# Sliding-window copy: twelve staged batches for eleven, engines offset by fours, last stores in parts

## The chip, the cores and the metric

The kernel runs on one core of one Trainium2 chip. The metric is device time in microseconds; the median of six runs before the change is 752.82 us (751.74 to 755.47). No arithmetic is done at all: the kernel only moves data, so the parts of the chip that matter are the sixteen DMA engines of the core, the HBM, and three queues from which DMAs are issued: SP's (q1 in the profile), ACT's (q10) and GpSimd's, called POOL (q0).

## The reference

```python
batch, length, dim = (32, 4096, 256)          # x, float32; window_size = 64, stride = 32
n_windows = (length - window_size) // stride + 1      # 127
result = np.zeros((batch, n_windows, window_size, dim), dtype=np.float32)
for i in range(n_windows):
    start = i * stride
    result[:, i] = x[:, start:start + window_size].copy()
```

A batch of x is 128 blocks of 32 rows, 32 KB each (4.194 MB). Window i is blocks i and i+1, 64 KB, so neighbouring windows overlap by half, and each block but the first and the last of a batch is written twice: as the second half of one window and as the first half of the next. The output is 32 x 127 windows, 266.3 MB.

## The kernel before

There are two ways to make a batch's windows.

**Direct** copies go from x to the output, DRAM to DRAM, each block read twice. `Copier.windows` (L34) copies n windows, whole (64 KB each, in pieces of 32 KB) or one half of each. SP issues groups of sixteen windows, seven groups to a batch. Such a group is sent either as one DMA of whole windows or as a pair of DMAs, all first halves and then all second halves. The bytes are the same; with pairs the queue holds one completion packet to each piece of 32 KB, with whole windows one to two.

**Staged** batches are read once into an SBUF tile of 128 partitions, one block to a partition (`Copier.load`, L51, 4.194 MB in pieces of 16 KB), and stored twice from there (`Copier.store`, L61), once as first halves and once as second halves. Each store writes 128 halves where a batch has only 127 windows, so one half at each edge falls into the neighbouring batch: its window there must be written again afterwards. `Staging` has six tiles in turn. `Staging.run` on ACT issues up to six loads, then their twelve stores, then the next group; a load waits for the stores that leave its tile, a store for its load. The staged batches are 1, 4, 7 and so on to 31, eleven; 31 is shifted by one block, so that it spills only backwards, into two windows of batch 30.

The loop over `direct` sends 147 groups on SP. A small calculation sets whether a group goes as a pair: `turns` counts packets of the queue, four for a pair and three for a whole group, and `share` adds 90/120 of a pair while ACT's turn number lies among the loads and 12/120 while it lies among the stores. Windows that don't make up a group of sixteen are the edges: 15 to a batch, on the side next to a staged batch, sent by POOL. POOL waits until the third last group on SP has landed (semaphore `near`) and, for each edge, until the staged neighbour's stores have landed (`wait_stored`). It ends with four windows and nine more as `columns` (L44, pieces of 4 KB, spread over all engines). SP's own last copy is `columns` for windows 125 and 126 of batch 30, which waits for all stores of the last staged batch. Then SP waits for all copies.

Of the kernel before, what the change touches and what calls it, by code (L numbers as in the profile page):

```python
# [11 lines left out]
class Copier:  # L12
# [36 lines left out]
    def load(self, q, t, b, shift):  # L49

        return q.dma_start(  # L51
            out=t[:, :],
            in_=self.xap(b * self.nb - shift, [[self.blk, self.nb], [1, self.blk]]),
            max_dma_last_dim=IN,
        )

    def store(self, q, t, b, half, shift):


        w = b * self.nw - half - shift  # L60
        return q.dma_start(  # L61
            out=self.oap(2 * w + half, [[2 * self.blk, self.nb], [1, self.blk]]),
            in_=t[:, :],
            max_dma_last_dim=OUT,
        )


class Staging:


    def __init__(self, c, tc, pool, dtype, batches, bufs, shifts):
        self.c, self.batches, self.shifts = c, batches, shifts
        self.tiles = [pool.tile([128, c.blk], dtype, name=f"xb{i}") for i in range(bufs)]
        self.loaded = [tc.alloc_semaphore(f"loaded{i}") for i in range(bufs)]
        self.stored = [tc.alloc_semaphore(f"stored{i}") for i in range(bufs)]

    def shift(self, g):
        return self.shifts.get(self.batches[g], 0)

    def load(self, q, g):  # L80
        n, i = divmod(g, len(self.tiles))
        if n:
            q.wait_ge(self.stored[i], 32 * n)
        self.c.load(q, self.tiles[i], self.batches[g], self.shift(g)).then_inc(self.loaded[i], 16)

    def store(self, q, g):
        n, i = divmod(g, len(self.tiles))
        q.wait_ge(self.loaded[i], 16 * (n + 1))
        for half in (0, 1):
            self.c.store(q, self.tiles[i], self.batches[g], half, self.shift(g)).then_inc(self.stored[i], 16)  # L90

    def wait_stored(self, q, g):
        n, i = divmod(g, len(self.tiles))
        q.wait_ge(self.stored[i], 32 * (n + 1))  # L94

    def run(self, q):
        bufs = len(self.tiles)
        for first in range(0, len(self.batches), bufs):
            group = range(first, min(first + bufs, len(self.batches)))
# [7 lines left out]
def kernel(  # L107
# [13 lines left out]
    staged = [*range(1, B, 3)]  # L121
    direct = [b for b in range(B) if b not in staged]
    pool = ctx.enter_context(tc.tile_pool(name="xb", bufs=1))

    st = Staging(c, tc, pool, x.dtype, staged, 6, {0: -1, B - 1: 1})
# [10 lines left out]
    per, loads, stores = 6, 6 * 17, 34  # L138
    todo = 7 * len(direct)
    turns = share = 0  # L140
    with tc.tile_critical():  # L141
        st.run(ring_s)

        for b in direct:
            w = 0 if b - 1 not in staged else 8 if b + 1 in staged and b + 1 < B - 1 else 15
            for j in range(7):
                todo -= 1
                sem = near if todo == 2 else done
                share += 90 if turns % (loads + per * stores) < loads else 12
                if share >= 120:  # L150
                    share -= 120
                    turns += 4
                    count(c.windows(ring_d, b, w, 16, 0), done)
                    count(c.windows(ring_d, b, w, 16, 1), sem)
                else:
                    turns += 3
                    count(c.windows(ring_d, b, w, 16), sem)
                w += 16
                if todo == 7:
                    count(c.windows(ring_d, B - 1, c.nw - 1, 1, 1, 2048), done)  # L160
                    if 0 in staged:
                        count(c.windows(ring_d, 0, 0, 1, 0, 2048), done)

        ring_r.wait_ge(near, 16)
        pieces = (32768,)
        last = B - 2
        for i, b in enumerate(direct[:-1]):
# [51 lines left out]
```

## Time and profile before

| | |
|---|---|
| median of the runs | 752.82 us |
| the profiled execution | 752.34 us |
| its span, from the first to the last instruction | 750.6 us |
| DMA packets, bytes | 18098, 313.26 MB, mean 417 GB/s |
| stores on ACT: number, median from issue to landing | 22, 143.4 us |
| loads on ACT | 11, 124.6 us |
| direct copies on SP: whole groups, halves | 96, 102 |
| first load, and first direct copy, issued at | 0.91 and 0.96 us |
| POOL's edges: first issued, issued after the wait for a store | 653.3 us, 703.6 us |

The profile gives the span in 40 slices with the rate of the DMA engines in each; queue rows give packets, megabytes and the time that the packets took, as a share of sixteen engines. A row of the view by stretches has the stretch, its length, POOL's busy time, the clock, the DMA share and GB/s. Packets are counted where they start, so that short stretches can show a share above 1 or a rate of zero while the engines work on. Packets under 512 B are the completions that count up a semaphore.

### The profile page before, as it was taken

What the parts mean: (1) busy time and instruction counts of PE and PEld (TensorE: products, weight loads), DVE (VectorE), ACT (ScalarE), POOL (GpSimd) and SP (SyncE); (2) the same over time, 40 slices, a digit from 0 to 9 for tenths busy, and PEclk for the clock granted to TensorE, in tenths of its full rate; (3) what the DMA queues carried; (4) which work ended last, traced back from release to release, by engine and by line L of the source; (5) the groups of instructions that cost most, each with busy time, mean ns of one, the idle gap of its engine ahead of it and who ended that gap; (6) DMA issues with size and microseconds to landing.
All of it is one profiled execution on the core that took longest, in us unless ns stands there. A gap on an engine that the chain in (4) does not pass through costs nothing.

```text
span 750.6 us, 309 instructions
## 1 busy us (share of the span) xinstructions
POOL 12.7 (2%) x26
## 2 busy tenths in 40 slices
POOL 0000000000000000000000000000000000130100
DMA  9999999999999999999999999999999999999996
GB/s 370 424 427 419 428 428 418 422 426 424 417 422 419 423 417 420 425 421 417 414 417 417 418 428 429 432 424 424 435 422 424 417 422 431 418 423 426 421 417 269
DMA packets 18098, 313.26 MB, mean 417 GB/s; under 512 B 4144, under 2 KB 4144, under 8 KB 4336
## 3 DMA queue, kind: packets, MB, share of 16 engines
q1 hardware_dynamic: 7952, 154.32, 48.7%
q10 hardware_dynamic: 8976, 138.41, 44.1%
q0 software_dynamic: 1168, 20.51, 6.5%
q14 instruction: 2, 0.02, 0.0%
HBM read 220.95 MB, written 267.09 MB: 650 GB/s over the span
## 4 chain that ended last, share of the span: by engine, by line
another core or an unknown queue 92%; POOL 2%; issue 0%; POOLq 0%; SPq 0%
POOL out_dram L34 2%; POOL out_dram L44 0%; POOLq L214 0%; POOLq L94 0%; SPq L141 0%
## 5 line engine op out<-in xcount | busy, mean ns | idle before, releaser
L34 POOL DMA_DIRECT2D out_dram<-in_x_dram x21 | 12.0, 575 | 692.9 <-DMA out_dram<-in_x_dram 652.8
L44 POOL DMA_DIRECT2D out_dram<-in_x_dram x1 | 0.6, 581 | 0.0
L200 POOL MEMSET const-float32-0.0<- 128x1 f32 x1 | 0.1, 98 | 0.2 <-issue 0.2
L200 POOL MEMSET const-bfloat16-1.0<- 128x1 bf16 x1 | 0.1, 102 | 0.0
L200 POOL MEMSET const-float32-1.0<- 128x1 f32 x1 | 0.1, 98 | 0.0
L200 POOL MEMSET const-uint8-127<- 128x1 uint8 x1 | 0.1, 98 | 0.0
## 6 DMA issues: line engine op xcount, KB each, us to landing
out_dram<-in_x_dram SPq DMA_DIRECT2D x96, 1024.0 KB, 101.8
out_dram<-xb ACTq DMA_DIRECT2D x22, 4096.0 KB, 143.4
out_dram<-in_x_dram SPq DMA_DIRECT2D x102, 512.0 KB, 90.6
xb<-in_x_dram ACTq DMA_DIRECT2D x11, 4096.0 KB, 124.6
out_dram<-in_x_dram POOLq DMA_DIRECT2D x20, 960.0 KB, 39.2
out_dram<-in_x_dram POOLq DMA_DIRECT2D x1, 576.0 KB, 41.1
out_dram<-in_x_dram POOLq DMA_DIRECT2D x1, 256.0 KB, 38.6
out_dram<-in_x_dram SPq DMA_DIRECT2D x1, 128.0 KB, 2.4
```

The lines of the kernel that those rows point to most:

```text
L34: return q.dma_start(out=self.oap((b * self.nw + w0) * 2 + h, [[2 * blk, n], row]), in_=self.xap(b * self.nb + w0 + h, [[blk, n], row]), m ...
L44: return q.dma_start(out=self.oap((b * self.nw + w0) * 2, [[part, 16], [2 * self.blk, n], row]), in_=self.xap(b * self.nb + w0, [[part, 16 ...
L200: nc = _bacc.Bacc("TRN2", target_bir_lowering=False, num_devices=1)
```

## The change

- Twelve batches are staged: 0, 3, 6, 9, 11, 14, 17, 20, 22, 25, 28, 31. Batch 0 is shifted so that it spills only forwards, and batch 31 as before. Batches 10 and 21 now lie between two staged ones and have two edges of 8 and 7 windows. Two single half windows, the first and the last of the output, are sent by SP half way.
- The first load goes as four DMAs of 32 partitions, every fourth one.
- A group on SP goes as a pair always during the turns of loads (and from eight turns ahead of the second group of loads), and in 89 of 120 cases during those of stores. `near` is now the second last group.
- The last direct group (batch 30, windows 96 to 111) is taken out of SP's list, and POOL sends it by `quarters`: copies of four windows (outermost dimension four), n of four 16 KB parts of each. Three of them, with 3, 2 and 1 parts of the first, second and third four windows, go at the very start; four more follow after the wait for `near`: all 4 parts of the fourth four windows, then the 1, 2 and 3 parts that the first three left.
- The last staged batch is stored as all second halves, then rows 0 to 31 of the first halves on the tile's semaphore, then rows 96 to 127 and four DMAs of 16 rows on a new semaphore, `ended`. SP's last `columns` waits for the tile's semaphore alone.
- POOL's last `columns` has ten windows where it had nine, and three windows go before it where four did.

```diff
@@ -46,21 +46,34 @@
             in_=self.xap(b * self.nb + w0, [[part, 16], [self.blk, n], row]),
         )
-    def load(self, q, t, b, shift):
-        return q.dma_start(
-            out=t[:, :],
-            in_=self.xap(b * self.nb - shift, [[self.blk, self.nb], [1, self.blk]]),
+    def quarters(self, q, b, w0, p0, n):
+        part = self.blk // 4
+        at = p0 * 2 * part
+        dims = [[part, 2 * n], [1, part]]
+        return q.dma_start(
+            out=bass.AP(self.out.tensor, self.oap((b * self.nw + w0) * 2, dims).offset + at, [[2 * self.blk, 4], *dims]),
+            in_=bass.AP(self.x.tensor, self.xap(b * self.nb + w0, dims).offset + at, [[self.blk, 4], *dims]),
+            max_dma_last_dim=4 * part,
+        )
+    def load(self, q, t, b, c, rows):
+        p, step, n, unit = rows
+        return q.dma_start(
+            out=t[p : p + (n - 1) * step + 1 : step, :],
+            in_=self.xap(b * self.nb + c + p // unit, [[step // unit * self.blk, n], [1, self.blk]]),
             max_dma_last_dim=IN,
         )
-    def store(self, q, t, b, half, shift):
-        w = b * self.nw - half - shift
-        return q.dma_start(
-            out=self.oap(2 * w + half, [[2 * self.blk, self.nb], [1, self.blk]]),
-            in_=t[:, :],
+    def store(self, q, t, b, c, rows, half):
+        p, step, n, unit = rows
+        w = b * self.nw + c + p // unit - half
+        return q.dma_start(
+            out=self.oap(2 * w + half, [[2 * step // unit * self.blk, n], [1, self.blk]]),
+            in_=t[p : p + (n - 1) * step + 1 : step, :],
             max_dma_last_dim=OUT,
         )
@@ -68,35 +81,53 @@
 class Staging:
-    def __init__(self, c, tc, pool, dtype, batches, bufs, shifts):
-        self.c, self.batches, self.shifts = c, batches, shifts
+    def __init__(self, c, tc, pool, dtype, items, bufs):
+        self.c, self.items = c, items
         self.tiles = [pool.tile([128, c.blk], dtype, name=f"xb{i}") for i in range(bufs)]
         self.loaded = [tc.alloc_semaphore(f"loaded{i}") for i in range(bufs)]
         self.stored = [tc.alloc_semaphore(f"stored{i}") for i in range(bufs)]
-    def shift(self, g):
-        return self.shifts.get(self.batches[g], 0)
+        self.ended = tc.alloc_semaphore("ended")
+        self.count = {sem: 0 for sem in (*self.loaded, *self.stored, self.ended)}
+        self.after_load, self.after_store = {}, {}
+    def issue(self, dma, sem):
+        dma.then_inc(sem, 16)
+        self.count[sem] += 16
     def load(self, q, g):
-        n, i = divmod(g, len(self.tiles))
-        if n:
-            q.wait_ge(self.stored[i], 32 * n)
-        self.c.load(q, self.tiles[i], self.batches[g], self.shift(g)).then_inc(self.loaded[i], 16)
+        i = g % len(self.tiles)
+        b, c, n = self.items[g]
+        if self.count[self.stored[i]]:
+            q.wait_ge(self.stored[i], self.count[self.stored[i]])
+        step = 128 // n
+        parts = [(k, 4, 32, 1) for k in range(4)] if g == 0 else [(0, step, n, step)]
+        for rows in parts:
+            self.issue(self.c.load(q, self.tiles[i], b, c, rows), self.loaded[i])
+        self.after_load[g] = self.count[self.loaded[i]]
     def store(self, q, g):
-        n, i = divmod(g, len(self.tiles))
-        q.wait_ge(self.loaded[i], 16 * (n + 1))
-        for half in (0, 1):
-            self.c.store(q, self.tiles[i], self.batches[g], half, self.shift(g)).then_inc(self.stored[i], 16)
+        i = g % len(self.tiles)
+        b, c, n = self.items[g]
+        q.wait_ge(self.loaded[i], self.after_load[g])
+        step = 128 // n
+        parts, end = [((0, step, n, step), 0), ((0, step, n, step), 1)], []
+        if g == len(self.items) - 1:
+            parts = [((0, 1, 128, 1), 1), ((0, 1, 32, 1), 0)]
+            end = [(96, 1, 32, 1)] + [(32 + k, 4, 16, 1) for k in range(4)]
+        for rows, half in parts:
+            self.issue(self.c.store(q, self.tiles[i], b, c, rows, half), self.stored[i])
+        for rows in end:
+            self.issue(self.c.store(q, self.tiles[i], b, c, rows, 0), self.ended)
+        self.after_store[g] = self.count[self.stored[i]]
     def wait_stored(self, q, g):
-        n, i = divmod(g, len(self.tiles))
-        q.wait_ge(self.stored[i], 32 * (n + 1))
+        q.wait_ge(self.stored[g % len(self.tiles)], self.after_store[g])
     def run(self, q):
         bufs = len(self.tiles)
-        for first in range(0, len(self.batches), bufs):
-            group = range(first, min(first + bufs, len(self.batches)))
+        for first in range(0, len(self.items), bufs):
+            group = range(first, min(first + bufs, len(self.items)))
             for g in group:
                 self.load(q, g)
             for g in group:
@@ -118,13 +149,14 @@
     n_win = (L - W) // S + 1
     assert out.shape == (B, n_win, W, D)
     c = Copier(x, out, B, L, D, W, S, n_win)
-    staged = [*range(1, B, 3)]
+    staged = [0, 3, 6, 9, 11, 14, 17, 20, 22, 25, 28, 31]
+    items = [(b, 1 if b == 0 else -1 if b == B - 1 else 0, c.nb) for b in staged]
+    place = {b: g for g, (b, _, n) in enumerate(items) if n == c.nb}
     direct = [b for b in range(B) if b not in staged]
     pool = ctx.enter_context(tc.tile_pool(name="xb", bufs=1))
-    st = Staging(c, tc, pool, x.dtype, staged, 6, {0: -1, B - 1: 1})
+    st = Staging(c, tc, pool, x.dtype, items, 6)
     ring_d, ring_s, ring_r = nc.sync, nc.scalar, nc.gpsimd
     done = tc.alloc_semaphore("done")
     near = tc.alloc_semaphore("near")
@@ -135,52 +167,66 @@
         dma.then_inc(sem, 16)
         total[sem] += 16
-    per, loads, stores = 6, 6 * 17, 34
-    todo = 7 * len(direct)
+    sixteens = []
+    for b in direct:
+        both = b - 1 in staged and b + 1 in staged
+        w = 8 if both else 15 if b - 1 in staged else 0
+        sixteens += [(b, w + 16 * j) for j in range((c.nw - w) // 16)]
+    apart = sixteens.pop()
+    singles = [(0, 0, 0), (B - 1, c.nw - 1, 1)]
+    edges = []
+    for b in direct[:-1]:
+        if b - 1 in staged and b + 1 in staged:
+            edges += [(b, 0, 8), (b, 120, 7)]
+        else:
+            edges.append((b, 0 if b - 1 in staged else 112, 15))
+    last = B - 2
+    edges.append((last, 112, 3))
+    first_loads, loads, stores = 6 * 17, 6 * 17, 6 * 34
     turns = share = 0
     with tc.tile_critical():
+        for k in range(3):
+            count(c.quarters(ring_r, apart[0], apart[1] + 4 * k, 0, 3 - k), rest)
         st.run(ring_s)
-        for b in direct:
-            w = 0 if b - 1 not in staged else 8 if b + 1 in staged and b + 1 < B - 1 else 15
-            for j in range(7):
-                todo -= 1
-                sem = near if todo == 2 else done
-                share += 90 if turns % (loads + per * stores) < loads else 12
-                if share >= 120:
-                    share -= 120
-                    turns += 4
-                    count(c.windows(ring_d, b, w, 16, 0), done)
-                    count(c.windows(ring_d, b, w, 16, 1), sem)
-                else:
-                    turns += 3
-                    count(c.windows(ring_d, b, w, 16), sem)
-                w += 16
-                if todo == 7:
-                    count(c.windows(ring_d, B - 1, c.nw - 1, 1, 1, 2048), done)
-                    if 0 in staged:
-                        count(c.windows(ring_d, 0, 0, 1, 0, 2048), done)
+        for i, (b, w) in enumerate(sixteens):
+            sem = near if i == len(sixteens) - 2 else done
+            second = turns - first_loads - stores
+            loading = turns < first_loads or 0 <= second < loads
+            share += 120 if turns < 28 or -8 <= second < 16 else 120 if loading else 89
+            if share >= 120:
+                share -= 120
+                turns += 4
+                count(c.windows(ring_d, b, w, 16, 0), done)
+                count(c.windows(ring_d, b, w, 16, 1), sem)
+            else:
+                turns += 3
+                count(c.windows(ring_d, b, w, 16), sem)
+            if i == len(sixteens) // 2:
+                for b, w, half in singles:
+                    count(c.windows(ring_d, b, w, 1, half, 2048), done)
         ring_r.wait_ge(near, 16)
-        pieces = (32768,)
-        last = B - 2
-        for i, b in enumerate(direct[:-1]):
-            for g, n in enumerate(staged):
-                if abs(n - b) == 1:
-                    st.wait_stored(ring_r, g)
-            parts = [(0, 15)] if b - 1 in staged else [(112, 15)]
-            if b - 1 in staged and b + 1 in staged:
-                parts = [(0, 8), (120, 7)]
-            for w, n in parts:
-                count(c.windows(ring_r, b, w, n, None, pieces[i % len(pieces)]), rest)
-        count(c.windows(ring_r, last, 112, 4), rest)
-        count(c.columns(ring_r, last, 116, 9), rest)
-        st.wait_stored(ring_d, len(staged) - 1)
+        for k, p in ((3, 0), (0, 3), (1, 2), (2, 1)):
+            count(c.quarters(ring_r, apart[0], apart[1] + 4 * k, p, 4 - p), rest)
+        for b, w, n in edges:
+            for k in (b - 1, b + 1):
+                if k in place and b != last:
+                    st.wait_stored(ring_r, place[k])
+            count(c.windows(ring_r, b, w, n), rest)
+        count(c.columns(ring_r, last, 115, 10), rest)
+        st.wait_stored(ring_d, place[B - 1])
         count(c.columns(ring_d, last, 125, 2), done)
-        for sem in (done, near, rest):
-            ring_d.wait_ge(sem, total[sem])
+        total[st.ended] = st.count[st.ended]
+        for sem, n in total.items():
+            ring_d.wait_ge(sem, n)
 # ---- launch: one core; inputs and outputs as the reference has them ----
```

## The prediction

> **What bounds the kernel now.** I read the page first: which engine is busy, what the DMA engines move, and what the queues cost.
>
> ```profile
> span 750.6 us, 309 instructions
> ...
> POOL 12.7 (2%) x26
> ...
> GB/s 370 424 427 419 428 428 418 422 426 424 417 422 419 423 417 420 425 421 417 414 417 417 418 428 429 432 424 424 435 422 424 417 422 431 418 423 426 421 417 269
> ...
> q1 hardware_dynamic: 7952, 154.32, 48.7%
> q10 hardware_dynamic: 8976, 138.41, 44.1%
> q0 software_dynamic: 1168, 20.51, 6.5%
> ...
> HBM read 220.95 MB, written 267.09 MB: 650 GB/s over the span
> ```
>
> No compute engine matters. q1 is SP's queue (direct copies), q10 ACT's (staged loads and stores), q0 POOL's (edges). Their shares add to 99.3%: the sixteen DMA engines never rest between the first slice and the last. Time is therefore bytes over rate, plus what is lost at both ends.
>
> Next, the rate by stretch (columns: stretch, its length, POOL busy, clock, DMA share, GB/s):
>
> ```profile
> 10.00:120.00 110.00, 0.00 (x0) 1.00 1.01 426
> 120.00:420.00 300.00, 0.00 (x0) 1.00 1.01 419
> 420.00:540.00 120.00, 0.00 (x0) 1.00 1.00 428
> 540.00:740.00 200.00, 12.55 (x22) 1.00 1.01 422
> 740.00:750.60 10.60, 0.00 (x0) 1.00 0.39 157
> ```
>
> From 10 to 740 us, (110x426 + 300x419 + 120x428 + 200x422)/730 = 422.3 GB/s. All 313.26 MB at that rate take 741.8 us, so both ends lose 8.8 us. The rate is not flat, and the DMA view of two stretches, 130 to 400 and then 420 to 540 us, says why (packets, MB, share):
>
> ```profile
> q1 hardware_dynamic: 3118, 65.51, 57.8%
> q10 hardware_dynamic: 3117, 48.19, 42.8%
> q1 hardware_dynamic: 1561, 27.33, 53.1%
> q10 hardware_dynamic: 1562, 24.02, 47.2%
> ```
>
> In the first, direct copies are 57.6% of the bytes, in the second 53.2%. A direct byte costs HBM twice (read and write), a staged one once: (2x65.51+48.19)/270 = 664 GB/s against (2x27.33+24.02)/120 = 656. The first moves 421 GB/s and the second 428. In the second a direct MB costs 0.531x120x16/27.33 = 37.3 engine-us against 38.1, a staged MB 37.7 against 38.4. So with much direct traffic HBM slows all packets by some 2%; with less, the engines' own pace is the limit. I infer two limits close together.
>
> Last, the ends. At 6.5 to 8.5 us the rate per half microsecond swings, as the engines change queue together:
>
> ```profile
> 6.50:7.00 0.50, 0.00 (x0) 1.00 0.00 0
> 7.00:7.50 0.50, 0.00 (x0) 1.00 1.22 524
> 7.50:8.00 0.50, 0.00 (x0) 1.00 2.12 918
> 8.00:8.50 0.50, 0.00 (x0) 1.00 0.30 131
> ```
>
> The zero is not idleness: packets count where they start, and all engines are inside one then. At the end, SP's wait for the last staged store and the rates behind it:
>
> ```profile
> SPq L44 <- DMA out_dram<-xb: 181.1, 1, 181.1
> 743.00:744.00 1.00, 0.00 (x0) 1.00 0.59 242
> 744.00:745.00 1.00, 0.00 (x0) 1.00 0.25 102
> 745.00:746.00 1.00, 0.00 (x0) 1.00 0.10 41
> 746.00:747.00 1.00, 0.00 (x0) 1.00 0.39 111
> ```
>
> The 128 KB of L44 on SP start at 745.2, when nearly everything else is done, and run alone at 746 to 747.
>
> [...] the pairs 3118/3117 and 1561/1562 agree exactly. [...]
>
> **The change, part by part.**
>
> *Bytes.* A staged batch is one 4.194 MB load and two such stores, 12.58 MB; a direct one is 127 windows of 65,536 B, 8.32 MB. Staged bytes become 12x12.583 = 151.00 (138.41 before), direct ones 20x8.323 and two single halves = 166.53 (154.32+20.51 before). The sum is 317.5 MB, 4.3 more: 10.2 us dearer at 422.3 GB/s. HBM traffic falls from 488.0 to 484.1 MB.
>
> *Turns.* For 16 windows an engine takes four packets if they go as two halves (two of data, two completions), three if whole; a load is 8 rows in two pieces and one completion, 17. The page confirms it: 33 staged DMAs x 17 x 16 = 8976. Before: SP 492 turns, POOL 1168/16 = 73, ACT 561. After, from the loop: 117 pairs and 22 whole copies, 534 turns; POOL's quarters 15, edges 58, columns 11; ACT 620 with its split load and stores. 534+84 and 7 for singles and SP's columns make 625 against 620. As before (570 against 561) both sides end together, so no queue is left to run alone, and POOL's edges, which wait for `near` and stores, get queued far ahead as now.
>
> *Mix.* Before, three pairs in four copies are sent during loads and one in ten during stores. After it is all pairs in loads and 74% in stores: the 53% mix of the 420 to 540 stretch, or less, for the whole run (52.4% over all). HBM demand at 429 GB/s is 1.524x429 = 654. Loads with pairs have been seen (428). Stores with mostly pairs are hardly seen: only about 520 to 540, at 426 to 430. For their rate the floor is what stores show now with 57% direct, 419 to 422, and the top the 432 of the best stretch. Extrapolating from 421 at 57.6% through 428 at 53.2% gives 429.3 at 52.4%. I take 429.5, the ceiling just above: 317.5/0.4295 = 739.3 us against 741.8. So 4.3 MB more are paid for, with 2.5 us to spare.
>
> *Engines apart.* Three early copies on POOL, 48, 32 and 16 KB per engine on three groups of four, none on the fourth; four later ones bring each to 64 KB. At 26.8 GB/s an engine (37.3 us a MB) 16 KB are 0.6 us, so the groups stand 0.6 us apart in the 2.4 us cycle of 64 KB. What that ends is the common swing above: 20 to 120 us moves 42.39 MB at 424 in spite of a low direct share, against 428 later; at most 1 us, and the 429.5 already assumes it. If the groups don't part, 1 us is lost.
>
> *Opening.* The ends' 8.8 us split as 2.3 ahead of 10 us and 6.5 after 740. The load in four DMAs lets SP's first descriptors in sooner, but the engines are already fed by ACT at 3.5 to 6 us (393 to 557 GB/s). Bounds: +0.3 (three more issues on ACT) to -0.9; I take -0.4.
>
> *Last stores.* SP's wait now ends after half 1 and a quarter of half 0; 96 rows, six an engine, follow behind it. The columns then run beside them instead of alone. Behind the waiting instruction on SP are only those columns and the final waits. About 1.2 us of lone transfer go, and part of the ragged decline from 743. What is late next is the last small store's completion, then the same closing 3 us (747.2 to 750.6). Bounds: +0.5 (five more DMAs with completions) to -2.5; I take -1.7.
>
> *Longer load group.* The second group has six loads instead of five, each waiting for its tile's stores. ACT's load at 383.8 is queued well before the 434.2 at which stores begin, so other loads cover the wait. If that cover went, one load is 20 us of ACT's queue, during which direct copies alone run against HBM; I take nothing.
>
> Sum: 739.3 + 8.8 - 0.4 - 1.7 = 746.0 span. The profiled execution took 752.34, 1.74 over its span: 747.7. The median of the runs is 0.48 above that execution: 748.2.
>
> **Rivals.**
> *The ceiling.* Pairs everywhere and engines apart hold the rate near the best stretch, 431.5: 735.8+6.3 = 742.1, hence 744.3. For it: 432 was reached twice with pairs; against: packets of loads beside pairs also gave 426.
> *A draw.* Stores beside direct copies slow at 427: 743.6+6.7 = 750.3, hence 752.5. For it: every stretch of stores has been at or under 423 for long; against: all of them carried whole copies.
> *The other side: bytes at an unchanged rate.* Twelfth staging costs its bytes, while the loss in store stretches comes from reading SBUF and writing HBM rather than from the mix. At 422.3 the data take 751.9, with 6.7 at the ends 758.6, hence 760.8. It decides from 425.5 downward: 746.2+6.7+1.74+0.48 = 755.1. For it: both queues' prices per MB differ by just 2% between stretches; against: 428 for 120 us with both loads and stores.
>
> **How the numbers follow.** A measurement here tells about 0.3% (2.3 us): faster is below 750.6, a rate over 428.1. Forecast 0.47 (746 to 751.5; 0.43 of it faster, 0.04 same), ceiling 0.19 faster, draw 0.18 same, bytes 0.16 slower. So 0.62, 0.22, 0.16. The range 744 to 756 leaves out the lowest of the ceiling (0.06) and most of the bytes case (0.12).
>
> **What would show it.** Rate from 10 to 740 us: 428 or more confirms the mix; stores after 130 us at 420 would refute it. q1 and q10 prices near 37.3 and 37.7 engine-us a MB. The half-microsecond swing at 7 us is gone if the engines part. SP's last columns start before the last packets on q10. I am wrong if the middle stays below 425.5, or if a queue runs out early and a stretch of one queue alone appears before 740.

## The result, and the profile after

The changed kernel takes 756.13 us (median of 15 runs, 755.41 to 757.06), the kernel before 752.84 in the runs beside it (34 runs, 751.32 to 757.04): a ratio of 1.0043, interval 1.0033 to 1.0052. It is slower by 3.3 us, where I had forecast 4.6 less; 756.13 also lies just outside the range. The profiled execution took 756.53 us with a span of 754.7. The page of the changed kernel:

```profile
span 754.7 us, 391 instructions
...
GB/s 360 419 432 432 431 428 431 434 430 428 434 426 436 429 432 430 432 432 431 426 422 431 431 428 431 432 431 432 432 435 430 432 432 434 424 412 429 422 393 188
DMA packets 20434, 317.56 MB, mean 421 GB/s; under 512 B 5840, under 2 KB 5840, under 8 KB 6064
...
q10 hardware_dynamic: 9920, 151.00, 47.0%
q1 hardware_dynamic: 8656, 145.97, 45.2%
q0 software_dynamic: 1856, 20.58, 7.0%
...
HBM read 216.86 MB, written 267.19 MB: 641 GB/s over the span
```

Each number of the row GB/s is the rate in one fortieth of the span. From the third slice to the 34th the rate is 426 to 436 with one slice at 422, where it was mostly 417 to 428. In the last six slices it is 412 to 429 and then 393 and 188. The view by stretches says the same (stretch, length, POOL busy, clock, DMA share, GB/s):

```profile
0.00:10.00 10.00, 2.13 (x7) 1.00 0.79 303
10.00:120.00 110.00, 0.00 (x0) 1.00 1.01 428
120.00:420.00 300.00, 0.00 (x0) 1.00 1.01 430
420.00:540.00 120.00, 0.00 (x0) 1.00 1.01 431
540.00:740.00 200.00, 15.28 (x27) 1.00 1.01 423
740.00:754.70 14.70, 0.00 (x0) 1.00 0.39 138
```

Stores after 130 us, which were at 419, now run at 430. The DMA view of 130 to 400 us gives the prices, the time of an engine that one MB takes: 0.527x270x16/60.89 = 37.4 engine-us for a direct MB and 0.478x270x16/55.17 = 37.4 for a staged one (before: 38.1 and 38.4).

```profile
q1 hardware_dynamic: 3571, 60.89, 52.7%
q10 hardware_dynamic: 3575, 55.17, 47.8%
```

Where the time went shows when it is cut in three: the middle is all bytes at the rate of 30 to 640 us (422.7 before, 430.5 after), the opening what the first 30 us lose against that rate (11.80 MB moved by then before, 11.40 after), the end the rest of the span.

| us | middle | opening | end | span |
|---|---|---|---|---|
| before | 741.1 | 2.1 | 7.4 | 750.6 |
| forecast | 739.3 | 1.9 | 4.8 | 746.0 |
| after | 737.7 | 3.5 | 13.5 | 754.7 |

Rows of 0 to 30 and 30 to 640 us, of the kernel before and then of the changed one:

```profile
0.00:30.00 30.00, 0.20 (x4) 1.00 0.94 393
30.00:640.00 610.00, 0.00 (x0) 1.00 1.01 423
```

```profile
0.00:30.00 30.00, 2.13 (x7) 1.00 0.94 380
30.00:640.00 610.00, 0.00 (x0) 1.00 1.01 431
```

The forecast's row has the ends as the prediction cut them, at 10 and 740 us; that cut gave the kernel before 8.8 us of ends, this one gives it 9.5.

So the middle brought 3.4 us for 4.3 MB more, the opening gave back 1.4 and the end 6.1. The end by stretches:

```profile
655.00:668.00 13.00, 8.62 (x16) 1.00 1.00 424
668.00:680.00 12.00, 0.00 (x0) 1.00 1.02 405
720.00:731.00 11.00, 0.00 (x0) 1.00 1.03 408
731.00:743.00 12.00, 0.00 (x0) 1.00 1.02 354
```

The last of these stretches in the kernel before:

```profile
731.00:743.00 12.00, 0.00 (x0) 1.00 0.97 405
```

And the DMA view of 655 to 668 us (packets, MB, share), of the changed kernel and then of the one before:

```profile
q10 hardware_dynamic: 325, 4.93, 88.5%
q0 software_dynamic: 326, 0.58, 11.7%
```

```profile
q0 software_dynamic: 112, 2.46, 45.0%
q10 hardware_dynamic: 138, 2.26, 41.9%
```

SP has nothing left at 655 us, and POOL's queue takes its place: 326 packets against ACT's 325, one for one as SP's 3571 and ACT's 3575 were from 130 to 400 us, but with 0.58 MB in them. Of them 255 are packets of 4 bytes; e1 below shows whose. A packet of one queue on one engine is a turn of that queue. ACT's queue gets ahead by 20 turns an engine here, while POOL's edges wait. It runs out at 731, and the last stretch is direct copies alone, at 354 GB/s:

```profile
q0 software_dynamic: 200, 4.07, 97.7%
q10 hardware_dynamic: 26, 0.18, 4.3%
```

SP's waits, last: the one for ACT's store is 27 us shorter than before (153.8 for 181.1), and SP's columns, issued at 722.9 instead of 745.2, run beside other packets as meant. Then SP waits for POOL's copies, and at the very end 2.4 us for POOL itself, where that row was 1.3. POOL has 30 DMAs instead of 22, but that isn't the whole of it: e15, with 22, has 1.7.

```profile
SPq L44 <- DMA out_dram<-xb: 153.8, 1, 153.8
SPq L229 <- DMA out_dram<-in_x_dram: 27.4, 1, 27.4
SPq L192 <- POOLq L192: 2.4, 1, 2.4
```

The last row as it was before:

```profile
SPq L141 <- POOLq L141: 1.3, 1, 1.3
```

No view names the engines. I take a packet that starts just when another ends to be of the same engine. Strung together so, the packets from 738 us on show when each engine ends (us; "closing" is from the last data to the end of the span):

```
                    median engine   last engine   SP's columns alone   closing
before                  744.0          746.0        to 747.2             3.4
after                   746            750.5        no                   4.2
```

### The profile page after: what moved, and what is told of

It is laid out like the page before. It is cut to its first block, busy times and chain, and to the rows that moved or that the text cites. A ratio compares the mean times of both kernels' runs of the same rounds, so it can differ in the third digit from the quotient of the medians.

```text
span 754.7 us, 391 instructions
## 1 busy us (share of the span) xinstructions
POOL 17.4 (2%) x34
## 3 DMA queue, kind: packets, MB, share of 16 engines
q1 hardware_dynamic: 8656, 145.97, 45.2%
q0 software_dynamic: 1856, 20.58, 7.0%
## 4 chain that ended last, share of the span: by engine, by line
another core or an unknown queue 90%; POOL 2%; issue 0%; PEldq 0%
POOL out_dram L34 1%; POOL out_dram L54 1%; POOL out_dram L44 0%; PEldq L260 0%
## 5 line engine op out<-in xcount | busy, mean ns | idle before, releaser
L54 POOL DMA_DIRECT2D out_dram<-in_x_dram x7 | 4.3, 624 | 648.2 <-DMA out_dram<-in_x_dram 647.1
L34 POOL DMA_DIRECT2D out_dram<-in_x_dram x22 | 12.3, 566 | 33.2 <-DMA out_dram<-xb 33.2
L44 POOL DMA_DIRECT2D out_dram<-in_x_dram x1 | 0.5, 548 | 0.0
```

Source lines behind the costliest of these rows:

```text
L34: return q.dma_start(out=self.oap((b * self.nw + w0) * 2 + h, [[2 * blk, n], row]), in_=self.xap(b * self.nb + w0 + h, [[blk, n], row]), m ...
L44: return q.dma_start(out=self.oap((b * self.nw + w0) * 2, [[part, 16], [2 * self.blk, n], row]), in_=self.xap(b * self.nb + w0, [[part, 16 ...
L54: return q.dma_start(out=bass.AP(self.out.tensor, self.oap((b * self.nw + w0) * 2, dims).offset + at, [[2 * self.blk, 4], *dims]), in_=bas ...
```

## The experiments

The chip isn't always the same, and that matters here: the kernel before takes 752.8 us beside the changed kernel, 754.6 beside e1 to e4, 755.1 beside e5 to e8, and 744.75 to 745.2 beside e9 to e18. The changed kernel differs too, by 2.4 us between its two chips (756.13, and 753.75 in e12). Ratios are to the kernel before on the same chip, us are medians. Comparisons are good within e1 to e4, e5 to e8, e9 to e11, e12 to e15 and e16 to e18, each of which shared a chip.

| run | us | ratio, 95% |
|---|---|---|
| e1 no quarters | 754.46 | 0.9995, 0.9981 to 1.0008 |
| e2 quarters midway | 757.19 | 1.003, 1.0019 to 1.0042 |
| e3 near earlier | 756.49 | 1.0024, 1.001 to 1.0037 |
| e4 last stores whole | 758.01 | 1.0046, 1.0031 to 1.0061 |
| e5, e6 (relief on e1) | 754.67, 754.9 | 0.9997, 0.9989 to 1.0005; 0.9994, 0.9983 to 1.0005 |
| e7 (relief on e2) | 756.99 | 1.0025, 1.0016 to 1.0033 |
| e8 opening whole (on e1) | 754.4 | 0.9995, 0.9985 to 1.0005 |
| e9, e10 | 754.72, 753.93 | 1.0124, 1.0111 to 1.0137; 1.0113, 1.01 to 1.0126 |
| e11, e13, e16: the mixture | 750.28, 750.79, 749.76 | 1.0069, 1.008, 1.0063 (±0.0014) |
| e12 changed kernel again | 753.75 | 1.0121, 1.0107 to 1.0135 |
| e14, e15: before, one part of the change | 745.87, 745.41 | 1.0013, 1.0005 to 1.0022; 1.0005, 0.9997 to 1.0013 |
| e17, e18 | 750.98, 750.78 | 1.0081, 1.0067 to 1.0095; 1.0073, 1.0061 to 1.0086 |

**e1: without the copies on four engines.** Their group goes on SP like all others.

```diff
-    apart = sixteens.pop()
-        for k in range(3):
-            count(c.quarters(ring_r, apart[0], apart[1] + 4 * k, 0, 3 - k), rest)
-        for k, p in ((3, 0), (0, 3), (1, 2), (2, 1)):
-            count(c.quarters(ring_r, apart[0], apart[1] + 4 * k, p, 4 - p), rest)
```

> The group of batch 30 that the four-engine copies carry goes on SP's list as an ordinary group; no such copies early or late. Theory A (the late four-engine copies take 36 turns of POOL's queue for little data, so ACT runs ahead at the handover and direct copies are left alone at the end): POOL's queue moves over 200 GB/s from 660 us on, no direct-only stretch after 730 us, 747 to 750 us; the first 100 us fall to about 424 GB/s as the engines are no longer apart. Theory B (the twelfth staged batch and its bytes cost the time, wherever the copies sit): 754 us or more, the direct-only stretch stays. Theory C (the last stores in parts let ACT end early): as B at the end, 754 or more.

e1 is 2.0 to 3.6 us faster than e2, e3 and e4 beside it, which keep the copies on four engines, and level with the kernel before. It isn't the 747 to 750 us of theory A, but A's signs are there: POOL's queue moves 252 GB/s, the stretch after SP's last packet keeps its rate, and no stretch of direct copies alone follows; stretches of e1, then its DMA view of 660 to 680 us:

```profile
660.00:680.00 20.00, 6.45 (x12) 1.00 1.02 431
720.00:730.00 10.00, 0.00 (x0) 1.00 1.01 411
730.00:740.00 10.00, 0.00 (x0) 1.00 0.98 415
```

```profile
q0 software_dynamic: 233, 5.05, 59.4%
q10 hardware_dynamic: 230, 3.57, 42.1%
```

q0's turns now carry 5.05 MB in 233 packets. The page of e1, for the row q0 of the changed kernel above:

```profile
q0 software_dynamic: 1232, 19.53, 6.2%
```

Its packets in the whole run fall by 624: 128 of data (8 KB each) and 496 of four bytes. These are not all completions. The trace records 480 increments of POOL's semaphore in the changed kernel and 368 in e1, sixteen for each of its 30 and 23 copies, so the seven copies account for 112. That the data of such a copy lie on four engines shows in the changed kernel's trace: packets of 8 KB start four at a time, every 0.91 us, from 655.3 to 659.5 us, and eight at a time from 659.6 to 662.2, where the next copy runs beside the first. The other 384 are three times the 128 packets of data: it is as if each of the twelve engines without data got as many packets of four bytes as each of the four with data carries. The same count, with the engines that a copy of n windows leaves out, gives the 64 such packets that the kernel before has beyond its increments (20 edges of 15 windows, one of four: 20x2 + 24), and exactly those of e1 (128), e9 and e10 (192) and e18 (256). So the three early copies are 15 turns an engine, which pass beside both other queues, and the four late ones 24, which delay direct copies alone.

The middle is no slower without these copies (429.5 GB/s from 30 to 640 us, as in e4 beside it), so setting the engines apart brought no rate, though the swing of half microseconds dies out sooner in the changed kernel (934, 131, 311, 426, 475 GB/s from 6.0 us on, where it was 459, 0, 524, 918, 131).

**e2: the four late copies midway**, when SP's 51st group has landed; **e3: POOL let go seven groups earlier.**

```diff
-            sem = near if i == len(sixteens) - 2 else done
+            sem = near if i == len(sixteens) - 2 else mid if i == 50 else done     # e2
+            sem = near if i == len(sixteens) - 9 else done                         # e3
...
-        ring_r.wait_ge(near, 16)
+        ring_r.wait_ge(mid, 16)                                                    # e2
         for k, p in ((3, 0), (0, 3), (1, 2), (2, 1)):
             count(c.quarters(ring_r, apart[0], apart[1] + 4 * k, p, 4 - p), rest)
+        ring_r.wait_ge(near, 16)                                                   # e2
```

> The four late copies go when SP's 51st group has landed, not after the third queue's wait near the end; the rest as in the changed kernel. Theory A: SP and ACT lose turns alike while POOL's small packets pass, so the end balances: 660 to 680 us at over 200 GB/s direct, no direct-only stretch, 745 to 748 us, and the middle stays at 430 GB/s. Theories B and C: 754 us or more.

> POOL is released seven groups earlier; its late copies run beside SP's last groups. Theory A: about 28 of SP's turns now lie beside POOL's 36, so ACT is ahead by 8 turns and not by 36: 746 to 750 us, the direct-only stretch shrinks to under 4 us. Theories B and C: within 1 us of 756.

In e2 the stretch of direct copies alone is gone; its DMA view of 731 to 743 us has both queues to the end:

```profile
q10 hardware_dynamic: 238, 2.75, 55.2%
q0 software_dynamic: 249, 2.18, 44.3%
```

Still it is 2.7 us slower than e1. Its engines end at some 744 in the median, all but one by 745.7, and one at 751.4; in e1 the median is also 744, the second last at 746.5, the last at 749.2. In e3 730 to 740 us move 374 GB/s, and one engine ends at 749.9 against a median of 744; its time is within 1 us of 756, as theories B and C had it. So the turn count alone isn't the cause: when it is mended, one engine is late, and neither run comes near the 745 to 750 us that theory A gave them.

**e4: the changed kernel with whole last stores.**

```diff
-        if g == len(self.items) - 1:
+        if g == len(self.items):
...
-        total[st.ended] = st.count[st.ended]
```

> The last staged batch is stored by two whole stores as in the kernel before, and SP's last columns wait for both. Theory A: the end is set by POOL's direct copies, so no gain or loss beyond 1 us against 756. Theory C: ACT's last stores end later and beside POOL's, 753 us or less.

The direct stretch stays (359 GB/s from 730 to 740, 264 in the ten after it). Its time is 758.01 where both theories had less, 1.9 us over the changed kernel; but that ran on another chip, where the ratio is the same (1.0043 for 1.0046). Whether the parts gain here isn't shown; e15 and e17 ask it without the copies on four engines.

**e5 to e7: is the highest-numbered engine the late one?** My guess, which no run shows, was that the sixteen engines take a DMA's rows in order of number. Then four last stores of 15 rows instead of 16 spare the highest one; the rows left go as a DMA of four rows (e6 spares it half as much, e7 is this on e2).

```diff
-            end = [(96, 1, 32, 1)] + [(32 + k, 4, 16, 1) for k in range(4)]
+            end = [(96, 1, 32, 1)] + [(32 + k, 4, 15, 1) for k in range(4)] + [(92, 1, 4, 1)]
```

> As the run without four-engine copies, and the last four stores of 16 rows go as 15 rows each, the four rows left in one DMA of four: [...]. Theory D (one engine is some 4 us behind the others over the run, its last stores end the program, and it is the one with the highest number): 2 to 3 us less than the run without four-engine copies (ratio to before 0.995 to 0.997). Rival E (the late engine is another one, or lateness comes from uneven shares of POOL's copies): no gain, up to 1.2 us more. Rival F (the end is set by queue order, not by an engine): within 0.5 us.

> The same with two of the four stores cut, [...]. Theory D: about 2.0 to 2.4 us less than without relief, nearly as much as the full dose. Rivals E and F: no gain.

> The four-engine copies in the middle of the run, as before, with the full relief of the last engine. There one engine ended 7 us after the median engine. Theory D: 3 to 5 us less than the 757.2 us (ratio 1.0030) of that run without relief. Rivals E and F: no gain.

None gains. In e5 one engine ends at 740.6, over 4 us ahead of the median, and must be the spared one. Another still ends at 749.1. So the spared engine isn't the late one, and theory D's gain is absent; no run shows which numbers the two have.

**e8: e1 with the first load in one DMA; e11, e13, e16: the same with 82 for 89** in the share of pairs, so that SP and POOL have 616 turns to ACT's 617 (e8: 621). I call this kernel the mixture.

```diff
-        parts = [(k, 4, 32, 1) for k in range(4)] if g == 0 else [(0, step, n, step)]
+        parts = [(0, step, n, step)]
...
-            share += 120 if turns < 28 or -8 <= second < 16 else 120 if loading else 89
+            share += 120 if turns < 28 or -8 <= second < 16 else 120 if loading else 82   # e11, e13, e16
```

> As the run without four-engine copies, with the first load as one DMA again. The bytes moved by 30 us were 11.3 MB there against 11.8 MB before. Theory G (the split load, not the pairs, costs these 0.5 MB or 1.2 us): 1 us less, 11.8 MB by 30 us. Rival H (the pairs of halves in the opening cost them): no gain, 11.3 MB.

> As the run with the opening load whole and no four-engine copies, with 82 in place of 89 of 120 pairs among the stores: six groups more go whole, six turns fewer for SP. With the load whole, 12.03 MB had moved by 30 us, 0.7 MB or 1.7 us more than with the load split, but direct copies were left for the end. If queue balance ate that gain, 1 to 2 us less than 754.4 (ratio 0.997 to 0.998). If the slow engine ate it, within 0.5 us of 0.9995.

The opening of e8; in e1 the second row reads 415:

```profile
0.00:10.00 10.00, 0.20 (x4) 1.00 0.80 315
10.00:30.00 20.00, 0.00 (x0) 1.00 1.04 444
```

By 30 us 12.03 MB are moved, against 11.3 in e1: the four DMAs cost 0.7 MB, 1.6 us (against e5 and e6 on its own chip, 11.4 and 11.5 MB, 1.3 to 1.5 us). Yet e8 is no faster than e5 and e6: its end is longer, and four turns of direct copies are left over. e11, where turns are equal, is 3.6 to 4.4 us under e9 and e10 beside it, but these differ in more than the opening (uneven copies midway, 89 pairs), and e8 ran on another chip. That equal turns keep the gain is therefore argued, not shown.

**e9, e10: which engine is late?** Midway POOL sends two groups of windows unevenly: a copy on four engines and one on twelve, with one rest over all sixteen (the helper `thirds`, 16 parts of 3 KB of four windows). I take each of POOL's copies to begin at the engine after the last one's, as the eight at a time in e1 above suggest, and both runs to begin at the same engine; no view names the engines. In e9 the first four of POOL's turn then get less, in e10 the last four.

```diff
+        for b, w in moved:                                             # e9
+            count(c.quarters(ring_r, b, w + 12, 0, 1), rest)
+            count(c.windows(ring_r, b, w, 12), rest)
+            count(c.thirds(ring_r, b, w + 12), rest)
```

> As the run without four-engine copies, but two groups of sixteen windows of batch 30 go through POOL in mid-run, each as a copy of four windows' first quarter (four engines), one of twelve windows (twelve engines) and the rest over all sixteen. If POOL's copies take engines in turn, the first four engines of its turn get 28 KB per group and the others 76 KB, so over two groups the first four are 96 KB behind the others in work: 2.7 us less than an even share, the others 0.9 us more. In the changed kernel the late engine stood among the four that the first four-engine copy had held up. Theory D2 (one slow engine, among those four, sets the end): 2 to 2.5 us less than the run without four-engine copies (ratio 0.9995 there), 0.996 to 0.997. Rival F (queue order sets the end): within 0.5 us of it. Rival E (the slow engine is elsewhere): 0.5 to 1 us more.

> The same two groups with the twelve windows first, so that the last four engines of POOL's turn are spared in the place of the first four. Theory D2: the slow engine gets 24 KB more, 0.5 to 1 us more than the run without four-engine copies, 1.0000 to 1.001. Rival F: as the run before this one. Rival E, if the slow engine is among the last four: 2 us less.

In both, four engines run some 3.5 us ahead from 290 us on, and the late one isn't among them: it is in neither four. The lead fits an order by turns: 96 KB less at 37.4 us a MB are 3.7 us, and copies that all began at one engine would put four engines 128 KB ahead of the next, 4.9 us. Their times say nothing of the theories, which were put against e1: that ran on another chip.

**e12, e13: the changed kernel and the mixture, side by side.**

> The changed kernel as it is, for comparison on the same chip as the next three. If its time is the engines' own pace and not HBM's, it is 755 to 757 us on any chip, whatever the kernel before takes there.

> The opening load whole, no four-engine copies, 82 of 120 pairs among the stores. On the chip where the kernel before took 745.2 us this one took 750.3. If it is engine-bound as well, 749 to 751 us here too, so that it beats the kernel before wherever that one takes 753 us or more (ratio 0.995), and the changed kernel by 5 to 6 us everywhere.

753.75 against 750.79: the copies on four engines, the split opening and the unequal turns together cost 3.0 us on this chip, not 5 to 6. The changed kernel is also faster than the 755 to 757 us that a pace of the engines alone was to give on any chip. And the kernel before takes 744.75 here, and both lose to it. In the mixture thirteen engines end by 741.4 and three at 743.9, 744.75 and 745.5.

**e14, e15: the kernel before with one part of the change each**, the first load in four DMAs, or the last stores in parts (rows as in the change, with the semaphore `ended`).

```diff
+        if g == 0:                                                     # e14
+            for k in range(4):
+                self.c.load_rows(q, self.tiles[i], self.batches[g], k).then_inc(self.loaded[i], 16)
+            return
...
+            self.c.store(q, self.tiles[i], b, 1, s).then_inc(self.stored[i], 16)          # e15
+            self.c.store_rows(q, self.tiles[i], b, s, 0, 1, 32).then_inc(self.stored[i], 16)
+            for p, step, n in [(96, 1, 32)] + [(32 + k, 4, 16) for k in range(4)]:
+                self.c.store_rows(q, self.tiles[i], b, s, p, step, n).then_inc(self.ended, 16)
```

> The kernel before with nothing changed but its first load, which goes as four DMAs of every fourth partition. Theory G [...]: some 0.7 MB less by 30 us, 1 to 2 us slower (ratio 1.0015 to 1.0025), with 16 KB packets of over 0.9 us in the first 30 us. Rival H (the split is harmless, pairs cost the opening): within 0.3 us.

> The kernel before with nothing changed but the stores of its last staged batch, in the parts of the changed kernel (all second halves, rows 0 to 31, rows 96 to 127, four times 16 rows). As forecast: 1.2 to 2.5 us faster, since SP's columns no longer run alone. Theory I ([...] the 16 KB packets take 1.2 us or more on some engines, which then end 4 us late): 1 to 3 us slower, with 16 KB packets over 0.9 us after 700 us, of which the kernel before has none.

The opening load in four costs 1.0 us by itself (0.4 to 1.6); stretches of e14, then of e15, which has it whole:

```profile
10.00:30.00 20.00, 0.00 (x0) 1.00 1.00 415
```

```profile
10.00:30.00 20.00, 0.00 (x0) 1.00 1.00 429
```

In these 20 us a packet takes 636 ns for 16 KB and 1257 for 32 KB in e14, 612 and 1215 in e15. Five packets of 16 KB take over 0.9 us from 5 to 30 us, none in e15, as theory G had it (in the first 5 us both kernels have such packets); its 0.7 MB are 0.3 here. On this kernel the last stores in parts bring nothing (+0.4 us, -0.2 to +1.0), neither the gain that was forecast nor the loss of theory I. And e15, whose middle is that of the kernel before, shows where this kernel is faster here, in its DMA view of 130 to 400 us:

```profile
DMA packets 6308, 115.29 MB, mean 427 GB/s; under 512 B 1302, under 2 KB 1302, under 8 KB 1302
...
q1 hardware_dynamic: 3157, 66.56, 58.0%
q10 hardware_dynamic: 3150, 48.73, 42.6%
```

At 57.7% direct bytes it moves 427 GB/s, where the chip of the first profile moved 421 at 57.6%. What the change buys in the middle (30 to 640 us, e15 and e12) is only 427.1 to 431.1 here, 0.9%, for 1.37% more bytes.

**e16, e17, e18.** e16 is the mixture again. e17 gives it whole last stores (77 for the 82, to keep the turns equal): do the last stores in parts stall packets? e18 adds to e17 the uneven copies of e9, so that of each group the second four of POOL's turn get 28 KB an engine and the others 76 KB (85 for the 77).

```diff
-        if g == len(self.items) - 1:
+        if g == len(self.items):                                       # e17, e18
...
+        for b, w in moved:                                             # e18
+            count(c.windows(ring_r, b, w, 4), rest)
+            count(c.quarters(ring_r, b, w + 4, 0, 1), rest)
+            count(c.windows(ring_r, b, w + 8, 8), rest)
+            count(c.thirds(ring_r, b, w + 4), rest)
```

> The opening load whole, no four-engine copies, 82 of 120 pairs: the measure for the next two. It took 750.3 and 750.8 us on two chips where the kernel before took 745. If its time is the engines' own pace, 750 to 752 us on any chip: a ratio of 1.007 to 1.008 where the kernel before takes 745, and of 0.994 to 0.997 where that one takes 753 or more.

> The mixture with the last staged batch stored by two whole stores, SP's columns behind both, and 77 of 120 pairs to keep the packet counts of both sides level. Theory I (32-row stores make two engines late): no 16 KB packets over 0.9 us after 700 us, fifteen engines end by 742 us, only the slow one near 744.5; then the columns alone, 1.2 us: about the same total, 749 to 751 us. Rival J (those long packets come from elsewhere, such as POOL's copies): they stay, and 752 us or more, since the columns now come last.

> The same, and two groups of batch 30 through POOL in mid-run so that the second four engines of its turn get 28 KB per group and the other twelve 76 KB. Theory D2 (the slow engine is among these four and sets the end): it ends about 2 us earlier, all engines within 2 us, 747 to 749 us, 1.5 to 2.5 us less than the run with whole last stores. Rival F (queue order sets the end): within 0.5 us of that run.

Stretches of e13 (the mixture), then of e17:

```profile
700.00:720.00 20.00, 2.21 (x4) 1.00 1.01 419
720.00:740.00 20.00, 0.00 (x0) 1.00 0.97 404
```

```profile
700.00:720.00 20.00, 2.21 (x4) 1.00 1.01 432
720.00:740.00 20.00, 0.00 (x0) 1.00 0.99 421
```

While the last stores in parts run, e13 has eleven packets of 16 KB that take 1.0 to 2.4 us instead of 0.61 (716 to 737 us, nine of them by 722, when the DMAs of 32 rows go; e16 eight, the changed kernel six), e17 none. But e17's columns on SP then go alone again, to 745.8, and its time is 1.2 us worse than that of e16 beside it (750.75 to 752.33 us, against 749.66 to 750.60). So in the mixture the parts do pay, in spite of the slow packets.

```
                    engines that end together   the others           SP's columns alone   closing
e13 (mixture)       13: 739.1 to 741.4          743.9, 744.75, 745.5  no                  3.7
e17 (whole stores)  15: 739.4 to 740.9          743.6                 to 745.8            3.4
e18 (spared)        16: 739.0 to 742.5          none                  to 745.0            4.1
```

In e18 no engine is late: at 617 us three engines are 3 us ahead of the other thirteen, so the fourth of the spared ones, the slow one, runs with the rest. It is in POOL's second four. The last engine ends 1.1 us earlier (742.5 for 743.6), but POOL's additional copies lengthen its closing from 3.4 to 4.1 us (SP's wait for POOL itself is 2.5, in e17 1.8), and of the 1.5 to 2.5 us expected 0.2 are left, within the noise.

## Why the prediction was wrong

**The middle: right.** 429.5 GB/s was forecast; 430.5 came from 30 to 640 us, with both prices at 37.4, half way to the 431.5 of the ceiling, which rests on the best 20 us of the kernel before:

```profile
460.00:480.00 20.00, 0.00 (x0) 1.00 1.01 432
```

Stores beside pairs, hardly seen before, run like loads beside pairs (430 GB/s from 120 to 420 us, 431 from 420 to 540). From 10 to 740 us, the stretch that the prediction named, the rate is 428, just its sign, because the failed end begins in there; by that cut the data take 742.0 us and the ends 12.7, so that 2.7 of the 8.7 us over the forecast span would count for the middle. "The other side: bytes at an unchanged rate" is refuted on the chip of the prediction, though the kernel did end on its side. On the chip of e12 to e15 it is nearer the truth (427.1 to 431.1): what the mix costs differs by chip, which a single profile couldn't tell. Why it differs isn't shown; that HBM slows the packets, as I had inferred, isn't either.

**The step that failed is the sum of the ends**, "8.8 - 0.4 - 1.7 = 6.7": they measure 3.5 + 13.5 = 17.0. (Its split "2.3 ahead of 10 us and 6.5 after 740" is 2.5 and 6.7 by the rows shown, a small matter.) Its terms:

- *"534+84 and 7 for singles and SP's columns make 625 against 620."* SP's part is exact, 541. Two summands of POOL's are wrong, "POOL's quarters 15, edges 58": they spread the data over sixteen engines and left out the packets of four bytes on the engines without data. With these the quarters are 624/16 = 39 turns and the edges 66, and the sum is 657 against 620 (from the page, (1856+8656)/16). The section on time and profile before calls all packets under 512 B completions; that is wrong by these packets. The trace has sixteen increments for each of POOL's copies, on few engines or all (480 for 30); the 384 other packets come on top. "No queue is left to run alone" was the conclusion, and "a stretch of one queue alone appears before 740" the sign named for being wrong; it is there, 731 to 743 at 354, and gone in e1 and e2. From the changed kernel to e1 the end falls from 13.5 to 9.8 us (span 752.9, middle 739.4, opening 3.7; on another chip): 3.7 us.
- *Opening: "I take -0.4".* Measured +1.0 us alone (e14); with pairs 1.3 to 1.6 us by the bytes moved (e8 against e5, e6 and e1), though not in the total time. SP's first packets did come sooner, at 2.40 us in the changed kernel and 5.78 before. But the upper bound of +0.3 counted the issues on ACT, not the rate of 10 to 30 us, which falls from 429 to 415 and with pairs from 444 to 415. In e14 packets of both queues take 3 to 4% longer then than in e15; why stays open.
- *Last stores: "I take -1.7".* Measured +0.4 with an interval about nothing in the kernel before (e15), and -1.2 in the mixture (e16 against e17). The gain is there in one kernel and not in the other, and nowhere as large as forecast. The columns were indeed alone no more, but what came next wasn't only "the last small store's completion": in the mixture the parts stall packets, eleven of 16 KB to 1.0 to 2.4 us for 0.61 in e13 and eight in e16, with none in e17, while the parts in e15 stall none over 0.87 us. What stalls them isn't shown; that the engines of e15 stand further apart is my guess.
- *What the sum didn't have: one engine is slower than the rest.* ACT's completions, sixteen to a DMA, show it: in e13, with no copy of POOL's in flight, fifteen engines are within 0.7 us at 635 us and the sixteenth is 4.6 us later, a gap that grows all the way, 0.6 to 0.7%. In the kernel before it is 3.8 us late, but the next is 3.4 late and the median 1.7: it hid in the spread. In e1 one engine ends alone, at 749.2, the second last at 746.5. Sparing the engine taken for the highest-numbered did nothing (ratios 0.9997 and 1.0025 in e5 and e7, 0.9995 and 1.003 without it), and sparing POOL's second four ended the lag (e18: all sixteen end from 739.0 to 742.5). No run names the engine's number, and the cause is open.
- *"Then the same closing 3 us".* 3.4 became 4.2; SP's wait for POOL within it went from 1.3 to 2.4.

Together: the ends exceed 6.7 by 10.3 us. The copies on four engines are 3.7 of it (e1, on another chip), the opening 1.6 (3.5 for 1.9), the last stores 0.5 to 2.1 by what they fell short of, and 0.7 is the other cut. What is left, 2.2 to 3.8 us, fits the late engine (2.7 us behind the second last in e1) and the longer wait for POOL (1.8 for 1.3). That is argued: e18, which freed the late engine, ended its engines 1.1 us earlier and gained 0.2. "Engines apart" was held to be in the 429.5 already, and brought no rate.

Open: why e2's last engine is 2.2 us later than e1's, with no stretch of direct copies alone in either; what slows the packets from 10 to 30 us; the slow engine; what sets the wait for POOL; why chips differ. No version beat both kernels on one chip: the mixture is 3.0 us under the changed one and 4.6 to 6.0 over the kernel before where that takes 745, and wasn't run where it takes 753 or more; e1, e5, e6 and e8 are level with the kernel before.

## What to carry to other kernels

Before two queues are made to end together, count every packet of each from a trace, the smallest too, and of a new form of copy above all: the queue of GpSimd's copies on four engines held 384 packets more than their data (128) and increments (112). When the mean rate is near the best stretch of the trace, as 430 GB/s is to 432 here, look at the spread of completions within one DMA: a slow engine can end last and alone (2.7 us behind the second last in e1), and no mean GB/s shows it. A better mix that is paid for in bytes gains only what the dearer mix really cost, and here that differed from chip to chip by as much as the gain (421 or 427 GB/s for the dearer mix).

## What was not expected of the hardware

- The same kernel takes 744.8 to 755.1 us by chip, while the changed one takes 753.75 and 756.13 on the two it ran on: with 57.7% direct bytes the middle moved 427 or 421 GB/s, with 52.5% it moved 430 and 431.
- A GpSimd copy on four engines counts its semaphore up by sixteen, and its queue holds besides three packets of four bytes for each of its data (384 for 128 in seven copies). They take turns like packets of 32 KB: 326 of that queue passed beside 325 of ACT's.
- Direct copies alone move 354 GB/s at the end of the changed kernel (341 in e12), beside stores 430.
- One of sixteen engines is 0.6 to 0.7% slower (e13); the others' packets in the middle take 1213 ns for 32 KB and 611 for 16 KB, its own 1221 and 613 (600 to 625 us of the changed kernel).
